# A two-layer decoder trunk on one core: all block inversions on POOL, value low parts on DVE, a recurrence in shorter hops

## The chip, the cores and the metric

One core of one Trainium2 chip runs the kernel. The metric is device time in microseconds of one execution, and lower is better; the time before is 2413.06 us, the median of 3 runs (2410.73 to 2416.13). The engines are PE (matrix products), DVE (vector), ACT (scalar functions), POOL (general) and SP, which here issues nearly all DMA transfers. Each engine has its own queue and works through it in order; an instruction that waits for a semaphore holds everything behind it on that engine.

## What is computed

The reference is a trunk of two layers over 512 tokens and 2048 channels, in float32. Layer 0 is forgetting attention (32 heads of 64), layer 1 is RWKV-7 time mixing with a state of 64x64 per head. Both have a gate by SiLU, an output projection and a residual. The part around the change is layer 1's recurrence:

```python
def step(S, inp):
    r_t, w_t, k_t, v_t, a_t, b_t = inp
    sa = jnp.einsum('bhvk,bhk->bhv', S, a_t)
    S = S * w_t[:, :, None, :] + sa[..., None] * b_t[:, :, None, :] \
        + v_t[..., None] * k_t[:, :, None, :]
    y_t = jnp.einsum('bhvk,bhk->bhv', S, r_t)
    return S, y_t
...
r, k, v, z = xr @ w_in[0], xk @ w_in[1], xv @ w_in[2], xg @ w_in[3]
v = v + (v_first - v) * jax.nn.sigmoid(v0 + (xv @ v1) @ v2)
...
return (y * jax.nn.silu(z)) @ w_out
```

The kernel does not step through 512 tokens. It works in chunks of 64 tokens. Within a chunk the dependence of the tokens on each other is a triangular 64x64 system per head, which is inverted beforehand; between chunks a state is handed on.

## The kernel before, in words

**Products.** Every large product is done in split precision: an operand is cut into a high part (`hi`, `whi`, made by ACT) and a low part (`lo`, `wlo`, made by DVE or POOL as source minus high part), and three streamed products replace one (high times high, low times high, high times low). Activations lie as 16 tiles of 128 channels x 512 tokens. An output tile of 128 channels takes 16 steps of 3 products into a PSUM bank `pj`. Its weights come in four parts of 4 steps (`raw`, 256 KB, three buffers; then `whi` and `wlo`, four buffers each), so one part feeds 12 products. SP loads a part, ACT and DVE split it, PE uses it.

**Layer 1's order on PE.** `backbone` (line 319) streams the output tiles: the rest of k, 16 of r, 16 of v (the values), 16 of z (the gate), 16 of the output projection. The first two tiles of each kind alternate. In what follows, V1 to V64 are the weight parts of the value tiles in the order of their use: V1 to V8 are tiles 0 and 1, V9 to V12 are tile 2, and so on.

**The planner.** `Flow` is a list of due tasks with a planned clock `fl.t`. Every PE product moves this clock on by its columns at 2400 per us (lines 91 to 96). All other work is written as tasks that run for a step, then `yield` how many units later the next step is due. So the program text of PE, DVE and ACT is laid down interleaved, in the order of the planned clock, and stays in that order on these three engines. SP's and POOL's queues are put in order by the framework's own scheduler, from the same text and its own notion of when something is ready.

**Mixed operands.** `mixed` (line 1114) makes the high and low part of one of the 16 activation tiles `hp` for the next kind of tile: `i` is 1 for r, 0 for the values, 2 for the gate. Line 1120 chooses the engine of the low part: for r and the values every second one goes to POOL.

**Inversions.** `keys` (line 1304) prepares one pair of heads, j = 0 to 15, and stores the triangular blocks to `mld`. After every fourth pair (a group, 4 in all) it starts `invert` and, later, `inverse` twice, for two pairs each. `invert` (line 1387) loads a group's 32x32 blocks as `lane`, one block per partition, and eliminates in 30 steps of two instructions (`lt`, then `lane`); POOL then masks, clears and stores the result to `qld`. In groups 0 to 2 POOL does the 30 steps in one go. Group 3 is in `DG`: DVE does them, spread over `DINV` = 32 units of the planner, and the two `inverse` tasks are due 40 and 52 units after the group's keys in place of 54 and 66. `inverse` (line 1409) reads `qld` back into `qt` (four loads on SP for each pair), turns blocks on DVE, joins them to 64x64 with small products on PE, and stores the result to `qtd`. The buffers of `qt` go round in fives.

**The recurrence.** `side` (line 1757) starts it when all 16 inverses are planned: `stage` loads the operands of two chunks (`rt`, `bk`, `prk`, `L`, `QP`, `SV`), `products` and `bonus` prepare them, and `recur` (line 1589) takes the 32 chunks of four groups of heads one after the other. A chunk is three hops: x from the state (copied by DVE to `xs`), times the inverse (copied by DVE to `SV`), then the new state (added by DVE). `hop` (line 1584) waits until the planned clock passes the next multiple of `HOP` = 3.9 units; between hops PE streams weights' products. `normed` finishes the output of two chunks and stores it to `ypd`, which the gate tiles read.

Of the kernel before, what the change touches and what calls it, by code (L numbers as in the profile page):

```python
# [12 lines left out]
OP = mybir.AluOpType  # L13
# [4 lines left out]
P = 128  # L18
# [113 lines left out]
def body(ctx, tc, a, out, dbg=None, stop=0):  # L132
    nc = tc.nc
    pe, act, dve, pool, sp = (InOrder(tc, e) for e in (nc.tensor, nc.scalar, nc.vector,
                                                       nc.gpsimd, nc.sync))
# [96 lines left out]
    def act_hi(hi, src):  # L232
        act.activation(hi, src, AF.Copy)
# [5 lines left out]
    def new_act(k):  # L239
        hi = cur["a"].tile([P, T], R, tag="hi", name="hi")  # L240
        lo = cur["a"].tile([P, T], R, tag="lo", name="lo")
        return hi, lo
# [46 lines left out]
    def silu_c(mp):  # L289
        cb = mp.tile([P, D], F, name="cb", bufs=1)  # L290
        cs = mp.tile([P, KT], F, name="cs", bufs=1)
        i = act.activation(cs, vecs[:, V_C], AF.Silu)
        return cb, cs, i
# [17 lines left out]
    def load(q, src, tag, shape=(P, T), bufs=None):  # L311
        t = q.tile(list(shape), F, tag=tag, name=tag, bufs=bufs)
        sp.dma_start(t, src)
        return t
# [81 lines left out]
    with ExitStack() as s0:  # L396
# [7 lines left out]
        with tc.tile_pool(name="st0", bufs=2, reuse_waits="tile") as q:  # L404
# [97 lines left out]
            cb, cs, i = silu_c(cbp)  # L502
# [95 lines left out]
        fl = Flow()  # L598
# [5 lines left out]
        q = sq0.enter_context(tc.tile_pool(name="at", bufs=2, reuse_waits="tile"))  # L604
# [318 lines left out]
        n = len(tiles)  # L923
# [112 lines left out]
    def col(v, j):  # L1036
        return vecs[:, v, j:j + 1]

    def c3(t):
        return t.rearrange("p (c t) -> p c t", c=NCH)  # L1040

    def u3(t):
        return t.rearrange("p (u t) -> p u t", u=NU)

    def of(d, j):

        return d[j // NJ][:, :, j % NJ]
# [3 lines left out]
    fl = Flow()  # L1051
# [7 lines left out]
    q = pools.enter_context(tc.tile_pool(name="kq", bufs=2, reuse_waits="tile"))  # L1059
# [24 lines left out]
    def need2(tag):  # L1084

        r = rings[tag]
        while any(r[i] > fl.t for i in range(max(0, len(r) - 2), len(r))):
            yield 0.1
        n = len(r)
        r[n] = r[n + 1] = 1e9  # L1090
        return n, n + 1

    def read(tag, n):
        rings[tag][n] = fl.t + 0.7
# [14 lines left out]
    def take(tag):  # L1109
        while not free[tag]:  # L1110
            yield 0.2
        free[tag] -= 1

    def mixed(i, to, old, k, m):
        while len(to) < k or k and (id(old), k - 1) not in spent:
            yield 0.1
        to.append(new_act(k))
        act_hi(to[k][0], m)
        yield 0.5
        e = pool if (k + 1) % (2, 2, 99)[i] == 0 else dve  # L1120
        e.tensor_tensor(out=to[k][1], in0=m, in1=to[k][0], op=OP.subtract)
        ready.add((id(to), k))
        free["m"] += 1
# [180 lines left out]
    def keys(q, j):  # L1304
        ip = q.tile([P, T], F, tag="ip", name="ip", bufs=2)
        sp.dma_start(u3(ip), of(ipd, j))
        kt = load(q, kTd[j], "kt", bufs=2)
        aa = load(q, aad[j], "aa", bufs=2)
        yield 8
        sq = q.tile([P, T], F, tag="sq", name="sq")  # L1310
        act.activation(sq, kt, AF.Square, scale=col(V_KK, j))
        yield from take("eI")
        eI = eIs[0]
        act.activation(eI[:, :, 1:], c3(ip), AF.Exp, scale=-EDEC)
        yield 2.2
        ss, n = yield from means(q, blkr, sq, "mh", "ml")
        yield 0.7
        t = q.tile([P, T], F, tag="t", name="t")
        act.activation(t, ss, AF.Relu, scale=2.0 ** 26, bias=nfloor)
        read("S", n)  # L1320
        act.activation(t, t, AF.Ln, bias=floor)
        act.activation(t, t, AF.Exp, scale=-0.5, bias=lnb)
        yield from take("eN")
        eN = q.tile([P, NCH, C], F, tag="eN", name="eN")
        act.activation(eN, c3(ip), AF.Exp, scale=EDEC)
        yield 2
        kk = q.tile([P, NCH, C], F, tag="kk", name="kk")
        dve.scalar_tensor_tensor(out=kk, in0=c3(kt), scalar=col(V_KK, j), in1=c3(t),
                                 op0=OP.mult, op1=OP.mult)
        at = q.tile([P, NCH, C], F, tag="at", name="at", bufs=2)  # L1330
        yield 0.7
        dve.scalar_tensor_tensor(out=at, in0=kk, scalar=-1.0, in1=eI[:, :, 0:C],
                                 op0=OP.mult, op1=OP.mult)
        free["eI"] += 1
        yield 0.7
        yield from take("bk")
        bk = q.tile([P, 2, NCH, C], F, tag="bk", name="bk")
        dve.tensor_tensor(out=kk, in0=kk, in1=c3(aa), op=OP.mult)
        yield 0.7
        dve.tensor_tensor(out=bk[:, 0], in0=kk, in1=eN, op=OP.mult)  # L1340
        yield 0.7
        act.activation(aa, aa, AF.Identity, scale=col(V_KA, j), bias=oka[:, j:j + 1])
        yield 0.8
        dve.tensor_tensor(out=kk, in0=c3(aa), in1=c3(kt), op=OP.mult)
        yield 0.7
        dve.tensor_tensor(out=bk[:, 1], in0=kk, in1=eN, op=OP.mult)
        free["eN"] += 1
        yield 1
        sp.dma_start(of(atd, j), u3(at.rearrange("p c t -> p (c t)")))
        for i in range(2):  # L1350
            sp.dma_start(bkd[j // NJ][:, :, i, j % NJ], u3(bk[:, i].rearrange("p c t -> p (c t)")))
        yield 1.5
        yield from take("gab")
        gab = q.tile([P, 2, 4, C], F, tag="gab", name="gab", bufs=12)
        ns = yield from need2("S")
        gs = [bank("S") for _ in ns]
        for c in range(4):
            for h in range(2):
                pe.matmul(gs[h][:, c * P:(c + 1) * P],
                          bk[HS[h], 0, 2 * c:2 * c + 2].rearrange("p c t -> p (c t)"),  # L1360
                          at[HS[h], 2 * c:2 * c + 2].rearrange("p c t -> p (c t)"),
                          start=True, stop=True)
        yield 0.7
        for h in range(2):
            g3 = gs[h].rearrange("p (c t) -> p c t", c=4)
            act.activation(gab[0:64, h], g3[0:64, :, 0:C], AF.Copy)
            act.activation(gab[64:128, h], g3[64:128, :, C:P], AF.Copy)
            read("S", ns[h])
            yield 0.7
        gabs[j] = gab  # L1370
        free["bk"] += 1
        yield 1.5
        for p in range(2):
            for b in range(2):
                r = 64 * p + 32 * b
                l = 32 * (j % 4) + 16 * p + 8 * b
                sp.dma_start(mld[j // 4, l:l + 8].rearrange("c s t -> s c t"),
                             gab[r:r + 32, :, :, 32 * b:32 * b + 32].rearrange(
                                 "s h c t -> s (h c) t"))
        md.add(j)  # L1380
        if j % 4 == 3:
            fl.start(fl.t + 1, invert(q, j // 4))
            for i in range(0, 4, 2):
                fl.start(fl.t + (DINV + 8 if j // 4 in DG else INV) + 6 * i,
                         inverse(q, (j - 3 + i, j - 2 + i)))

    def invert(q, grp):
        yield 3
        while not md >= set(range(4 * grp, 4 * grp + 4)):
            yield 0.2  # L1390
        m = q.tile([P, 32, 32], F, tag="lane", name="lane", bufs=2)
        sp.dma_start(m, mld[grp])
        for s in range(1, 31):
            n = 31 - s
            t = q.tile([P, s, n], F, tag="lt", name="lt")
            e = dve if grp in DG else pool
            e.tensor_tensor(out=t, in0=m[:, 0:s, s:s + 1].broadcast_to([P, s, n]),
                               in1=m[:, s:s + 1, s + 1:].broadcast_to([P, s, n]),
                               op=OP.mult)
            e.tensor_tensor(out=m[:, 0:s, s + 1:], in0=m[:, 0:s, s + 1:], in1=t,  # L1400
                            op=OP.add)
            if grp in DG:
                yield DINV / 30
        pool.affine_select(out=m, in_=m, pattern=[[-1, 32], [1, 32]],
                           compare_op=OP.is_ge, fill=0.0, base=-1, channel_multiplier=0)
        pool.memset(m.rearrange("p s t -> p (s t)")[:, 0:1024:33], 1.0)
        pool.dma_start(qld[grp], m)
# [176 lines left out]
    def hop():  # L1584
        n = fl.t // HOP
        while fl.t // HOP == n:
            yield 0.1
# [162 lines left out]


    STW = 5
    DG, DINV = (3,), 32
    HOP = 3.9
    INV, KEY = 54, 9.8

    def side(q):
# [102 lines left out]
```

## Time and profile before

| what | us |
|---|---|
| median of 3 runs | 2413.06 |
| the profiled execution, its own time | 2413.1 |
| its span, first to last instruction | 2411.2 |
| PE busy in the span | 2308.0 |
| DVE, ACT, POOL busy | 1605.5, 1257.2, 686.2 |
| granted clock of PE, mean | 0.982 |

A span is divided into what each engine does; an engine that is not the bottleneck may idle at no cost. In the profile nearly all instructions have line L90, since one helper records them, so they are told apart by their tiles (`out<-in`). A wait row reads: who waited, for whom, total us, times, longest. In a timeline row the first number is the start, the second the duration, and the square brackets hold the engine's idle time before it and what ended that. Some matmul records can be missing.

### The profile page before, as it was taken

What the parts mean: (1) busy time and instruction counts of PE and PEld (TensorE: products, weight loads), DVE (VectorE), ACT (ScalarE), POOL (GpSimd) and SP (SyncE); (2) the same over time, 40 slices, a digit from 0 to 9 for tenths busy, and PEclk for the clock granted to TensorE, in tenths of its full rate; (3) what the DMA queues carried; (4) which work ended last, traced back from release to release, by engine and by line L of the source; (5) the groups of instructions that cost most, each with busy time, mean ns of one, the idle gap of its engine ahead of it and who ended that gap; (6) DMA issues with size and microseconds to landing.
All of it is one profiled execution on the core that took longest, in us unless ns stands there. A gap on an engine that the chain in (4) does not pass through costs nothing. (4 is left out here: it accounts for less than half of the span.)

```text
span 2411.2 us, 39377 instructions
## 1 busy us (share of the span) xinstructions
PE 2308.0 (96%) x13626; PEld 1807.8 (75%) x13626; DVE 1605.5 (67%) x2850; ACT 1257.2 (52%) x2300; POOL 686.2 (28%) x1114
## 2 busy tenths in 40 slices
PE   6999899999999999998999898899999999999999
PEld 4787677877778778886777676677777777777787
DVE  6886678888888745335797567667477776765322
ACT  4435655555565544225646777764345556665221
POOL 0002332533324210110042207771245535450000
PEclk8999999999999999999999999989999999999999
DMA  8864366666666456444755999886867766644543
GB/s 304 329 224 158 108 198 216 212 216 222 201 222 213 133 181 205 137 147 141 227 183 185 301 270 278 262 253 192 237 184 198 212 177 189 173 132 153 160 137 96
DMA packets 388151, 480.22 MB, mean 199 GB/s; under 512 B 146032, under 2 KB 217840, under 8 KB 384112
## 3 DMA queue, kind: packets, MB, share of 16 engines
q1 hardware_dynamic: 386288, 475.08, 63.4%
q0 software_dynamic: 1664, 2.63, 0.3%
q8 instruction: 108, 1.77, 0.3%
q14 instruction: 91, 0.75, 0.1%
HBM read 381.63 MB, written 95.95 MB: 198 GB/s over the span
## 5 line engine op out<-in xcount | busy, mean ns | idle before, releaser
L90 PE MATMUL pj<-hi,whi 128*128 128x512 f32 x2416 | 987.5, 409 | 14.2 <-ACT hi L90 8.2
L90 PE MATMUL pj<-hi,wlo 128*128 128x512 f32 x2416 | 960.2, 397 | 9.1 <-DVE wlo L90 9.1
L90 PE MATMUL pj<-lo,whi 128*128 128x512 f32 x2416 | 960.1, 397 | 0.0
L90 DVE TENSOR_TENSOR wlo<-raw,whi 128x512 fp32r<-128x512 f32 (+2 forms) x628 | 474.5, 763 | 261.4 <-ACT whi L90 258.0
L90 ACT ACTIVATE whi<-raw 128x512 fp32r<-128x512 f32 (+2 forms) x628 | 394.2, 634 | 405.2 <-PE pj L90 229.3
L90 PEld LDWEIGHTS pj<-hi,whi 128*128 128x128 f32 x2416 | 459.6, 190 | 120.4 <-ACT hi L90 9.0
L90 PEld LDWEIGHTS pj<-lo,whi 128*128 128x128 f32 x2416 | 458.4, 190 | 108.7 <-DVE lo L90 0.6
L90 PEld LDWEIGHTS pj<-hi,wlo 128*128 128x128 f32 x2416 | 460.1, 190 | 105.1 <-DVE wlo L90 12.4
L90 DVE CUSTOM_DVE_ANT_0 wm<-wm,cb 128x1024 f32<-128x1024 f32 x128 | 156.7, 1225 | 0.3
L90 POOL TENSOR_SCALAR SV<-SV,dec 64x64 f32<-64x64 f32 x224 | 93.4, 439 | 105.9 <-DVE SV L90 71.7
L90 ACT ACTIVATE pr<-Sm,mx 128x128 f32<-128x128 f32 (+3 forms) x128 | 71.5, 558 | 85.6 <-POOL mx L90 81.6
L90 POOL TENSOR_SCALAR mx<-mx 128x1 f32<-128x1 f32 x128 | 65.7, 513 | 154.9 <-DVE mx L90 118.0
L90 POOL TENSOR_SCALAR pr<-pr,rc 128x128 f32<-128x128 f32 (+3 forms) x128 | 87.6, 685 | 33.0 <-DVE rc L90 28.6
L90 POOL TENSOR_TENSOR lt<-lane 128x30 f32<-128x30 f32 (+14 forms) x90 | 62.7, 697 | 83.9 <-DMA lane<-mld 77.1
L90 DVE CUSTOM_DVE_ANT_0 Sm<-S,cmask 128x128 f32<-128x128 f32 (+3 forms) x128 | 62.0, 484 | 36.0 <-PE S L90 35.4
L90 POOL TENSOR_TENSOR bk<-bk,eI 128x512 f32<-128x512 f32 x32 | 36.1, 1128 | 112.3 <-PE S L90 75.3
L90 POOL TENSOR_TENSOR lane<-lane,lt 128x30 f32<-128x30 f32 (+14 forms) x90 | 65.7, 730 | 7.1
L90 PE MATMUL S<-k,q 128*128 128x128 f32 (+7 forms) x256 | 62.4, 326 | 0.0
L90 PE MATMUL tr<-ident,pr 128*128 128x128 f32 x320 | 57.2, 277 | 4.3 <-DVE pT L90 1.4
L90 POOL TENSOR_TENSOR acc<-acc,sq 128x512 f32<-128x512 f32 x14 | 18.1, 1295 | 150.8 <-ACT sq L90 150.8
L90 PEld LDWEIGHTS tr<-ident,pr 128*128 128x128 f32 x320 | 41.6, 142 | 25.4 <-ACT pT L90 6.9
L90 DVE SCALAR_TENSOR_TENSOR hp<-pj,gate,hp 128x512 f32<-128x512 f32 x16 | 12.0, 751 | 68.9 <-PE pj L90 68.9
(325 smaller groups left out, 3272.8 us busy)
## 6 DMA issues: line engine op xcount, KB each, us to landing
wm<-in_wmodT SPq DMA_DIRECT2D x132, 512.0 KB, 4.3
raw<-in_wz SPq DMA_DIRECT2D x128, 256.0 KB, 3.8
raw<-in_wo SPq DMA_DIRECT2D x128, 256.0 KB, 3.5
raw<-in_wv SPq DMA_DIRECT2D x124, 256.0 KB, 3.8
wm<-in_wmodT SPq DMA_DIRECT2D x30, 1024.0 KB, 6.9
raw<-in_wk SPq DMA_DIRECT2D x96, 256.0 KB, 3.7
raw<-in_wr SPq DMA_DIRECT2D x64, 256.0 KB, 5.1
raw<-in_wq SPq DMA_DIRECT2D x56, 256.0 KB, 3.6
```

The source lines that it names most:

```text
L90: self.last = f(*a, **k)
```

## The change

Three things change. Every group's inversion is done by POOL in one go, so the table `DG`, its spread `DINV` and the shorter due time of group 3's inverses are gone; these are due 54 and 66 units after the keys, like the other groups'. The low parts of the values' operand are all made on DVE; r's are still shared. And `HOP` is 3.6 units in place of 3.9.

```diff
@@ mixed
-        e = pool if (k + 1) % (2, 2, 99)[i] == 0 else dve
+        e = pool if i == 1 and k % 2 else dve
@@ keys
-                fl.start(fl.t + (DINV + 8 if j // 4 in DG else INV) + 6 * i,
-                         inverse(q, (j - 3 + i, j - 2 + i)))
+                fl.start(fl.t + INV + 6 * i, inverse(q, (j - 3 + i, j - 2 + i)))
@@ invert
-            e = dve if grp in DG else pool
-            e.tensor_tensor(out=t, in0=m[:, 0:s, s:s + 1].broadcast_to([P, s, n]),
+            pool.tensor_tensor(out=t, in0=m[:, 0:s, s:s + 1].broadcast_to([P, s, n]),
                                in1=m[:, s:s + 1, s + 1:].broadcast_to([P, s, n]),
                                op=OP.mult)
-            e.tensor_tensor(out=m[:, 0:s, s + 1:], in0=m[:, 0:s, s + 1:], in1=t,
-                            op=OP.add)
-            if grp in DG:
-                yield DINV / 30
+            pool.tensor_tensor(out=m[:, 0:s, s + 1:], in0=m[:, 0:s, s + 1:], in1=t,
+                               op=OP.add)
@@ constants
-    DG, DINV = (3,), 32
-    HOP = 3.9
+    HOP = 3.6
```

Two places of the new order follow. First DVE, where group 3's inversion begins; `lo` is a low part of the values' operand, `wlo` of a weight part. Before:

```order
L90 TENSOR_TENSOR wlo<-raw,whi 128x512
L90 TENSOR_TENSOR lt<-lane 128x30
L90 TENSOR_TENSOR lane<-lane,lt 128x30
L90 TENSOR_TENSOR lo<-hp,hi 128x512
L90 TENSOR_TENSOR wlo<-raw,whi 128x512
L90 TENSOR_TENSOR lt<-lane 128x58
L90 TENSOR_TENSOR lane<-lane,lt 128x2x29
L90 TENSOR_TENSOR lt<-lane 128x84
L90 TENSOR_TENSOR lane<-lane,lt 128x3x28
L90 TENSOR_TENSOR lo<-hp,hi 128x512
```

Now:

```order
L90 TENSOR_TENSOR wlo<-raw,whi 128x512
L90 TENSOR_TENSOR lo<-hp,hi 128x512
L90 TENSOR_TENSOR wlo<-raw,whi 128x512
L90 TENSOR_TENSOR lo<-hp,hi 128x512 x2
L90 TENSOR_TENSOR wlo<-raw,whi 128x512
```

The 60 steps are gone from DVE and stand in one piece on POOL, right behind group 2's store to `qld`, where eight `lo` stood; those eight are now on DVE.

Second SP, around group 3's reads of `qld`. `qt_13171` and `qt_13174` are the buffers of pairs 12 and 13 here, `qtd<-qt_13174` and `qtd<-qt_13177` store pairs 8 and 9, and the three `raw` in the first row are V8 to V10. Before:

```order
L90 DMA raw<-in_wv 128x512 x3
L90 DMA qtd<-qt_13174 128x512
L90 DMA qtd<-qt_13177 128x512
L90 DMA hp<-mxd 128x512 x3
L90 DMA raw<-in_wv 128x512
L90 DMA qt_13171<-qld 32x8x32 x4
L90 DMA qt_13174<-qld 32x8x32 x4
L90 DMA sv<-svd 128x512
L90 DMA raw<-in_wv 128x512 x2
```

Now:

```order
L90 DMA raw<-in_wv 128x512 x3
L90 DMA qtd<-qt_13174 128x512
L90 DMA qtd<-qt_13177 128x512
L90 DMA qt_13171<-qld 32x8x32 x3
L90 DMA raw<-in_wv 128x512 x2
L90 DMA qt_13171<-qld 32x8x32
L90 DMA qt_13174<-qld 32x8x32 x4
L90 DMA qt_13177<-qld 32x8x32
L90 DMA sv<-svd 128x512
L90 DMA raw<-in_wv 128x512
```

V11 stood ahead of the first read of `qld` and stands behind it now, though the same inverse is due later on DVE, where its first turned block moves from behind V13's low part to behind V17's.

On PE the recurrence's first product with `QP` stands 60 streamed products later than before, and the last step of its last chunk 69 earlier.

## The prediction

> **What bounds the kernel now.** I read the page first, then the chain of waits, then the waits of the matmul engine (PE) by stretch, then each engine's timeline where the change acts. The page's list of engines:
>
> ```profile
> PE 2308.0 (96%) x13626; PEld 1807.8 (75%) x13626; DVE 1605.5 (67%) x2850; ACT 1257.2 (52%) x2300; POOL 686.2 (28%) x1114
> ```
>
> The last long piece of the chain of waits (start, length, what, how many):
>
> ```profile
> 2237.22 170.14 PE pj L90 x728
> ```
>
> PE is busy 96% of 2411.2 us, and the change gives PE as many rows as before, 10,262, so only PE's pauses can change: 103 us in all. Undisturbed, a streamed product (128x512, into bank pj) costs 170.14/728 = 0.234 us. Three stretches matter: the last group's inversion (1612 to 1660), the recurrence (1735 to 2203), the end of the gate tiles (2203 to 2238). One or more rows of PE's waits from each, in that order (total us, times, longest):
>
> ```profile
> PE pj L90 <- DVE wlo L90: 6.1, 4, 1.7
> ```
>
> ```profile
> PE S L90 <- ACT GP L90: 8.3, 5, 4.1
> PE S L90 <- ACT mhi L90: 3.9, 1, 3.9
> ...
> PE x L90 <- DVE SV L90: 0.9, 1, 0.9
> PE x L90 <- DVE xs L90: 0.6, 1, 0.6
> ```
>
> ```profile
> PE pj L90 <- DVE wlo L90: 3.0, 4, 1.4
> ```
>
> In the inversion PE waits for DVE. In the recurrence it waits mostly for ACT emptying score banks, and only 0.9 + 0.6 us for the recurrence's own copies (SV, xs). Busy time by stretch, with columns stretch, length, then PE, weight loads, DVE, ACT, POOL, granted clock, DMA share, GB/s:
>
> ```profile
> 1617.00:1629.00 12.00, 8.95 (x26) 6.49 (x26) 11.62 (x25) 3.88 (x8) 3.07 (x3) 0.72 0.76 247
> 1640.00:1652.00 12.00, 8.24 (x85) 5.67 (x84) 11.53 (x26) 4.65 (x9) 1.42 (x1) 0.86 0.63 178
> 1652.00:1677.00 25.00, 25.00 (x287) 20.14 (x286) 15.39 (x35) 10.54 (x22) 2.29 (x4) 1.00 0.75 207
> 1735.00:2203.00 468.00, 450.98 (x4374) 352.96 (x4374) 320.23 (x683) 264.43 (x455) 207.47 (x394) 0.99 0.63 176
> ```
>
> In the first two DVE is full, PE pauses 3.05 and 3.76 us, and the clock falls: half clock for (1-0.72)x2 = 56% of 12 us is 6.7 us, and (1-0.86)x2 of 12 is 3.4. In the third PE never pauses. In the recurrence it pauses 17 us.
>
> **Part 1: the last inversion and half the low parts change places.** What DVE loses, on its timeline:
>
> ```profile
> 1616.55 0.19 DVE L90 TENSOR_TENSOR lt<-lane 128x30 f32<-128x30 f32 x1 [10.02 <-DMA lane<-mld]
> ...
> 1617.48 1.76 DVE L90 TENSOR_TENSOR wlo<-raw,whi 128x512 fp32r<-128x512 f32 x1
> ```
>
> and on PE's:
>
> ```profile
> 1619.30 0.50 PE L90 MATMUL pj<-hi,wlo 128*128 128x512 f32 x1 [1.38 <-DVE wlo L90]
> ...
> 1621.94 0.80 PE L90 MATMUL pj<-hi,wlo 128*128 128x512 f32 x1 [1.67 <-DVE wlo L90]
> ...
> 1623.38 0.63 PE L90 MATMUL pj<-hi,wlo 128*128 128x512 f32 x1
> 1623.81 0.63 PE L90 MATMUL pj<-lo,whi 128*128 128x512 f32 x1
> ```
>
> DVE's queue is in order. Its first inversion instruction waits 10.02 us for the lane load, with the weights' low part (wlo) behind it; PE then stops at 1619.30 and 1621.94. After that products start 0.43 us apart instead of 0.234, so 6.7 us of half clock hold about 15 products and cost 15x0.2 = 3.0 us; 3.4 us cost 1.5. Stage total: 3.05 + 3.76 + 3.0 + 1.5 = 11.3 us. It is of DVE's making: the block, 60 small instructions, and a wlo that takes 1.76 us while a low part runs on POOL. In the change DVE carries 16 low parts there and no inversion. I take 11 us as removed up to 1652 (bounds 5, if weight loads that come late there stay late, and 11.3).
>
> **Where it goes next.** The inversion now lasts as long as POOL makes it, and SP waits for its result. The tile `lane` (minimum/median/maximum ns, first and last start; the last row is its loads and stores):
>
> ```profile
> L90 DVE TENSOR_TENSOR lt<-lane x30: 191/329/1497, 1616.5 to 1657.5; 128x30 f32<-128x30 f32 x2, 128x58 f32<-128x58 f32 x2, 128x84 f32<-128x84 f32 x2, 128x108 f32<-128x108 f32 x2
> ...
> DMA to landing us min/median/max: 5.1/6.0/7.8
> ```
>
> POOL's timeline, first step and end of groups 0 and 2:
>
> ```profile
> 1455.62 0.24 POOL L90 TENSOR_TENSOR lt<-lane 128x30 f32<-128x30 f32 x1 [69.70 <-DMA lane<-mld]
> ...
> 1505.54 1.60 POOL L90 TENSOR_SCALAR_AFFINE_SELECT lane<-lane 128x1024 f32<-128x1024 f32 x1
> ...
> 1565.93 0.23 POOL L90 TENSOR_TENSOR lt<-lane 128x30 f32<-128x30 f32 x1 [7.38 <-DMA lane<-mld]
> ...
> 1610.66 1.26 POOL L90 TENSOR_SCALAR_AFFINE_SELECT lane<-lane 128x1024 f32<-128x1024 f32 x1
> ```
>
> SP's waits from 1611 to 1700, and its queue:
>
> ```profile
> SPq L90 <- DMA qld<-lane: 4.4, 2, 3.0
> ```
>
> ```profile
> 1657.74 1.11 SPq L90 DMA_DIRECT2D qtd<-qt  x2
> ...
> 1664.92 3.78 SPq L90 DMA_DIRECT2D qt<-qld  x8
> 1668.79 0.40 SPq L90 DMA_DIRECT2D sv<-svd  x1
> 1669.29 0.86 SPq L90 DMA_DIRECT2D raw<-in_wv  x2
> ```
>
> POOL takes 1505.5-1455.6 = 49.9 us for group 0 and 44.7 for group 2. Group 3 starts when the lane data is there, 1616.5 as now. I take group 2's 44.7, nearest in time and in DVE's load: 1661.2; then 1.26 for the masking and 0.5 (taken) for a clearing and the store's issue; the store to qld 5.1, the least, as DMA is light while SP waits: landed at 1668.1. Bounds: DVE's own length now, 41.2, gives 1664.6; 49.9 and a store of 7.8 give 1676. Now it lands at 1664.9, when SP's wait of 3.0 us ends.
>
> Most of this inverse is emitted 14 planner units later, but the order shows that SP's first three reads of qld are not: they stand one weight load EARLIER, ahead of part V11 (the third part of value tile 2's weights). SP stores qtd as soon as PE and ACT have done group 2's first pair, 11 us before 1657.74, and then stands at qld for some 20 us with V11 and all later loads behind it. PE, 11 us ahead, runs dry. The rows for that: PE's first product of V11, a high part on ACT, DVE's product with sv for value tile 1, and the page's row of these loads (KB, us to landing).
>
> ```profile
> 1676.70 0.40 PE L90 MATMUL pj<-hi,whi 128*128 128x512 f32 x1
> ```
>
> ```profile
> 1668.27 0.63 ACT L90 ACTIVATE whi<-raw 128x512 fp32r<-128x512 f32 x1
> ```
>
> ```profile
> 1671.65 0.69 DVE L90 TENSOR_TENSOR vf<-vf,sv 128x512 f32<-128x512 f32 x1 [0.67 <-DMA sv<-svd]
> ```
>
> ```profile
> raw<-in_wv SPq DMA_DIRECT2D x124, 256.0 KB, 3.8
> ```
>
> PE starts V11 at 1676.70 now. In the change: landing 1668.1, three reads at 3.78/8 = 1.4 us, load 3.8, high part 0.63, low part 0.69 (a DVE pass of that shape), 0.3 between them: 1674.9. Without the wait PE would come at 1676.7-11 = 1665.7, so it stands for 9.2 us; of the 11 us only 1.8 remain. The clock falls after such a pause, and between the 3.0 and 1.5 above I take 1.8. Sum of part 1: -11 + 9.2 + 1.8 = 0. Bounds: -4.5 (landing 1664.6, so 5.7 stood, clock 0.8) and +9 (landing 1676, 17.1 stood, clock 3.0). V12 has a second wait before it: the load sv for value tile 1 comes after six more reads, and DVE's product with sv stands ahead of V12's low part. Landing 1668.1, nine reads 4.3, two weight loads 0.9, sv 2.9 (1668.79 to 1671.65), two DVE passes 1.4: 1677.6, when PE needs it (1674.9 + 12x0.234 = 1677.7). Nothing more is lost there.
>
> The rows of wlo beside an inversion on POOL (1455 to 1505) and without one (1660 to 1735), and one POOL step twice:
>
> ```profile
> L90 DVE TENSOR_TENSOR wlo<-raw,whi x14: 691/1038/1192, 1454.3 to 1504.6; 128x512 fp32r<-128x512 f32 x14
> ```
>
> ```profile
> L90 DVE TENSOR_TENSOR wlo<-raw,whi x23: 678/692/710, 1660.6 to 1733.0; 128x512 fp32r<-128x512 f32 x23
> ```
>
> ```profile
> 1587.55 0.62 POOL L90 TENSOR_TENSOR lt<-lane 128x240 f32<-128x240 f32 x1
> ...
> 1589.03 0.95 POOL L90 TENSOR_TENSOR lt<-lane 128x240 f32<-128x240 f32 x1
> ```
>
> Some 30 low parts in the stage cost DVE 0.35 us more each, 10 us beside the 21 of the passes themselves, in 44 us: no path. The other way round, POOL's step is 0.62 or 0.95 us. Once SP holds the loads back DVE has nothing to do, and POOL's last 20 us shrink by up to a third, 6 us: landing at 1662, rival B. [...]
>
> **Part 2: the recurrence.** It starts 60 products later and ends 69 earlier in PE's order (1,047 products between its steps become 918). Its second product, first and last start:
>
> ```profile
> L90 PE MATMUL x<-xs,QP x512: 221/222/369, 1754.1 to 2188.4; 128*64 128x64 f32 x171
> ```
>
> 31 chunks take 434.3 us, so one of a chunk's 3 hops takes 4.67 us; 3.6/3.9 of it is 4.31, and DVE has 0.36 us less to answer. It is late in only 2 of some 95 steps now (0.9 and 0.6). I take the same again, +1.5; bounds 0 (nothing gets late) and +9 (a quarter of 95 steps lose 0.36). The other 15 us there come from ACT's queue, where the exponentials of 16 stages stand for their loads; there are still 16: 0, bounds -6 and +6. The earlier end cannot give more than the 3.0 us lost after 2203, and that wait falls in the last gate tiles, after the recurrence is over: 0.
>
> **Sum.** The profiled execution took 2413.1 us (span 2411.2 and 1.9 around it), like the median 2413.06. 2413.1 + 0 + 1.5 = 2414.6; I say 2414.5.
>
> **Rivals.** *A, the stage's gain stays whole:* the wait at qld does not bind, because weights are loaded further ahead of PE than I count. For: PE does not pause from 1652 to 1677 though SP waits 3.0 us there. Against: three load buffers and four split ones hold seven parts, 84 products, 20 us, and part of them is used up when SP's wait begins. 2413.1 - 11 + 1.5 = 2403.6. Chance 0.15.
>
> *B, POOL runs free while DVE is empty:* landing at 1662, PE stands 9.2-6.1 = 3.1 us, clock 1: 2413.1 - 11 + 3.1 + 1 + 1.5 = 2407.7. For: the 0.62 row. Against: over half of the inversion is done before DVE empties. Chance 0.17.
>
> *C, slower, SP is held longer:* one mechanism, SP's wait for qld; from a landing at 1668 on every us is a us of PE. With group 0's 49.9 and a 7.8 us store it is +9, and with 1.5 for the hops 2423.6; the middle of the case is 2421. For: group 0 took that long. Against: DVE had more to do then. Chance 0.17.
>
> *D, slower, the shorter hop decides:* once a quarter of the steps miss, +9, 2422. For: DVE is busy 320 of 468 us there. Against: two late steps of 95 now. Chance 0.11.
>
> **How the numbers follow.** Forecast, no change: 0.40. A measurement of this kernel tells 0.2% (4.8 us) from no change. Faster: A and B, 0.32, of which 0.03 fall within 0.2%: 0.29. Slower: C and D, 0.28. Within: 0.43. The likeliest case alone: 2409 to 2419. The range for 8 in 10 reaches from below A to above C and D: 2402 to 2425.
>
> **What would show it.** Right: SP's wait for qld<-lane grows to over 10 us; PE pauses 5 to 10 us between 1660 and 1676 on whi or wlo; no pause of PE from 1617 to 1650; DVE's block of 10.02 us is gone. Wrong: qld lands before 1660, or PE runs through that stretch (A, B); PE's waits for xs and SV pass 5 us (D). I would also be wrong if ACT's stands in the recurrence changed by over 6 us, which the order does not settle.

## The result and the profile after

The change takes 2431.93 us (median of 4 runs, 2430.28 to 2432.96), before 2412.93 beside it: ratio 1.0085, 95% interval 1.0073 to 1.0097. It is 19 us slower, outside the predicted range of 2402 to 2425. The profiled execution took 2431.0 us, span 2429.0. PE, from the page:

```profile
PE 2313.1 (95%) x13626; PEld 1813.1 (75%) x13626; DVE 1600.1 (66%) x2798; ACT 1255.8 (52%) x2300; POOL 712.2 (29%) x1166
```

PE has the same instructions as before, yet it is busy 5.1 us longer (a slower clock, 0.980 in place of 0.982) and pauses 115.9 us in place of 103.2, 12.7 more. Both together are the 17.8 us by which the span grew. Busy time by stretch says where (columns as in the prediction: stretch, length, PE, weight loads, DVE, ACT, POOL, granted clock, DMA share, GB/s):

```profile
1617.00:1629.00 12.00, 11.23 (x49) 8.80 (x48) 8.65 (x10) 6.92 (x13) 10.74 (x17) 1.00 0.82 273
1640.00:1652.00 12.00, 12.00 (x163) 9.32 (x163) 6.19 (x9) 4.25 (x11) 10.77 (x16) 0.87 0.56 142
1652.00:1677.00 25.00, 20.75 (x201) 16.70 (x200) 9.97 (x16) 7.58 (x16) 7.98 (x17) 0.86 0.52 144
1735.00:2203.00 468.00, 437.44 (x4292) 339.79 (x4291) 324.86 (x686) 257.59 (x444) 211.93 (x403) 0.97 0.62 171
2203.00:2238.00 35.00, 35.00 (x152) 28.20 (x151) 17.71 (x32) 18.88 (x30) 0.00 (x0) 1.00 0.56 176
```

In the stage of the last inversion DVE is no longer full, and PE's loss has moved to the third row. The recurrence carries the result: PE pauses 468-437.4 = 30.6 us there, 17.0 before, and the clock is 0.97 in place of 0.99. After 2203 the 3.0 us of pauses are gone.

**The stage.** PE's waits from 1612 to 1677:

```profile
PE x L90 <- ACT us L90: 4.2, 1, 4.2
PE pj L90 <- ACT r L90: 2.8, 1, 2.8
PE pj L90 <- DVE wlo L90: 1.8, 3, 0.8
```

The timelines of SP, ACT and PE where the longest of them ends:

```profile
1663.43 1.31 SPq L90 DMA_DIRECT2D qt<-qld  x3
1664.83 0.87 SPq L90 DMA_DIRECT2D raw<-in_wv  x2
```

```profile
1668.47 0.63 ACT L90 ACTIVATE whi<-raw 128x512 fp32r<-128x512 f32 x1 [6.41 <-DMA raw<-in_wv]
1669.13 0.78 ACT L90 ACTIVATE us<-x 32x256 f32<-32x256 f32 x2
```

```profile
1669.55 1.46 PE L90 MATMUL x<-qt,us 32*32 32x32 f32 x32 [4.16 <-ACT us L90]
```

And SP's wait for the inverse, from 1600 to 1700:

```profile
SPq L90 <- DMA qld<-lane: 10.7, 1, 10.7
```

Up to ACT's `whi` this is the predicted chain: SP stands at `qld` until 1663.43, makes three reads, and only then issues V11. ACT's high part of V11 waits 6.41 us for it, with the copy `us` behind it in ACT's queue, and PE waits for `us`.

**The recurrence.** PE's waits from 1735 to 2203, and its second product per chunk:

```profile
PE S L90 <- ACT vt L90: 11.1, 3, 4.7
PE S L90 <- DVE mlo L90: 5.5, 6, 2.0
PE S L90 <- DVE vf L90: 5.0, 2, 4.1
PE x L90 <- DVE xs L90: 2.9, 2, 1.9
PE S L90 <- ACT GP L90: 2.7, 4, 1.2
PE S L90 <- ACT sq L90: 1.0, 2, 0.7
PE x L90 <- DVE SV L90: 0.9, 2, 0.7
```

```profile
L90 PE MATMUL x<-xs,QP x512: 221/222/271, 1768.7 to 2194.9; 128*64 128x64 f32 x171
```

The waits for DVE sum to 14.3 us, before to 3.8 (`SV` 0.9, `xs` 0.6, and two rows that the prediction does not show):

```profile
PE S L90 <- DVE mlo L90: 1.8, 4, 0.6
```

```profile
PE S L90 <- DVE vf L90: 0.5, 1, 0.5
```

Those for ACT are 14.8, before 12.2. A hop takes (2194.9-1768.7)/93 = 4.58 us, not 4.31; before it took 4.67. All of the waits for `mlo` and `vf` in the change fall in the first half of the stretch, while the value tiles still run. That half, before and then in the change:

```profile
1735.00:1969.00 234.00, 220.23 (x2170) 172.37 (x2170) 174.22 (x365) 120.29 (x222) 111.15 (x212) 0.97 0.72 195
```

```profile
1735.00:1969.00 234.00, 209.63 (x1989) 161.69 (x1989) 168.03 (x346) 110.23 (x204) 106.77 (x202) 0.95 0.67 181
```

PE pauses 24.4 us there in place of 13.8, although DVE is busy for less time than before, 168.0 us in place of 174.2. What DVE did ahead of the longest wait for it:

```profile
1893.65 1.42 DVE L90 SCALAR_TENSOR_TENSOR prk<-rt,vecs,bk 64x128 f32<-64x128 f32 x4
1895.10 0.88 DVE L90 COPY SV<-x 64x256 f32<-64x256 f32 x2
1896.01 0.71 DVE L90 SCALAR_TENSOR_TENSOR prk<-rt,vecs,bk 64x128 f32<-64x128 f32 x2
1896.75 1.14 DVE L90 SCALAR_TENSOR_TENSOR dc<-dc,vecs,sq 128x128 f32<-128x128 f32 x4
1897.81 1.14 DVE L90 SCALAR_TENSOR_TENSOR dc<-dc,vecs,bv 128x128 f32<-128x128 f32 x4
...
1902.74 0.69 DVE L90 TENSOR_TENSOR vf<-vf,pj 128x512 f32<-128x512 f32 x1
```

```profile
1903.57 1.09 PE L90 MATMUL S<-ident,vf 128*128 128x128 f32 x4 [4.09 <-DVE vf L90]
```

From 1892 to 1904 DVE works with hardly a gap, through recurrence copies, side work of the stages (`prk`, `dc`) and a value tile (`vf`), while PE waits at the head of its own queue for the last of it. Such a run is not by itself what stops PE: the kernel before has a longer one, and PE works right through it.

```profile
1783.00:1805.00 22.00, 22.00 (x233) 17.56 (x232) 21.30 (x45) 11.16 (x21) 13.77 (x27) 1.00 0.75 198
```

### The profile page after: what moved, and what is told of

It is laid out like the page before. It is cut to its first block, busy times and chain, and to the rows that moved or that the text cites. A ratio compares the mean times of both kernels' runs of the same rounds, so it can differ in the third digit from the quotient of the medians.

```text
span 2429.0 us, 39369 instructions
## 1 busy us (share of the span) xinstructions
PE 2313.1 (95%) x13626; PEld 1813.1 (75%) x13626; DVE 1600.1 (66%) x2798; ACT 1255.8 (52%) x2300; POOL 712.2 (29%) x1166
## 5 line engine op out<-in xcount | busy, mean ns | idle before, releaser
L90 POOL TENSOR_TENSOR lt<-lane 128x30 f32<-128x30 f32 (+14 forms) x120 | 81.6, 680 | 90.9 <-DMA lane<-mld 81.7
L90 POOL TENSOR_TENSOR lane<-lane,lt 128x30 f32<-128x30 f32 (+14 forms) x120 | 85.9, 715 | 9.4
L90 DVE TENSOR_TENSOR lo<-hp,hi 128x512 fp32r<-128x512 f32 x54 | 43.4, 809 | 36.2 <-ACT hi L90 34.9
```

Source lines behind the costliest of these rows:

```text
L90: self.last = f(*a, **k)
```

## The experiments

All are read against the kernel before, run beside them on the same chip. The differences are of medians; the change itself stands at +19.0.

| run | what differs | us | against before | ratio, 95% |
|---|---|---|---|---|
| e1 | before, hop 3.6 | 2427.47 | +15.2 | 1.0041 to 1.0067 |
| e2 | change, hop 3.9 | 2443.90 | +31.7 | 1.0112 to 1.0138 |
| e3 | before, low parts on DVE | 2409.60 | -2.6 | 0.9977 to 0.9996 |
| e4 | before, inversion on POOL, later start | 2447.36 | +35.1 | 1.0126 to 1.0154 |
| e5 | change less 64 us of DVE work | 2412.49 | +1.1 | 0.9993 to 1.0013 |
| e6 | before less the same 64 us | 2403.70 | -7.7 | 0.9954 to 0.9979 |
| e7 | before, later start alone | 2438.86 | +27.4 | 1.0103 to 1.0138 |
| e8 | change, hop 3.7 | 2434.09 | +22.7 | 1.0085 to 1.0115 |
| e9 | change, 8 gate low parts on POOL | 2432.84 | +21.9 | 1.0076 to 1.0103 |
| e10 | e3, 29 us of DVE work done by POOL | 2428.69 | +17.8 | 1.0055 to 1.0087 |
| e11 | e3, hop 3.75 | 2421.44 | +10.5 | 1.0028 to 1.0053 |
| e12 | e3, hop 4.05 | 2431.61 | +20.7 | 1.0076 to 1.0103 |
| e13 | change less 46 us (`prk`) | 2415.88 | +5.1 | 1.0010 to 1.0028 |
| e14 | change less 18 us (`dc`) | 2420.08 | +9.3 | 1.0024 to 1.0051 |
| e15 | change, hop 3.9, old start | 2413.36 | +2.6 | 1.0005 to 1.0024 |

### Which of the parts: e1 to e4

e1 is the kernel before with the short hop; e2 the changed kernel with the old one, the same two lines the other way round:

```diff
-    HOP = 3.9
+    HOP = 3.6
```

e3 is the kernel before with the low parts on DVE; in e4, which is e2 otherwise, this line is the old one again:

```diff
-        e = pool if (k + 1) % (2, 2, 99)[i] == 0 else dve
+        e = pool if i == 1 and k % 2 else dve
```

> The kernel before with nothing changed but the hop, 3.6 planner units apart in place of 3.9 (start of the recurrence, inversions and low parts as before). The traces say that up to the recurrence the two kernels are level and that the 19 us arise inside it: from product 5283 to 6600 PE's pauses grow from 20.0 to 30.6 us and what it loses at half clock from 6.9 to 14.2 us. Theory H, the shorter hop is the cause: +15 to +19 us against before. Rival I, the later start is the cause (the side work of the recurrence is squeezed at its start): within 4 us of before. Rival O, each new order of the side work falls differently: anything from -10 to +15.

> The changed kernel with the hop back at 3.9 units; inversions on POOL, low parts on the vector engine and the later start stay. Theory H: within 4 us of before (part 1 by itself came out level in the traces: PE loses 36.5 us from product 4700 to 5283 before and 36.7 after). Rival I: +15 to +19 us, as the full change. Rival O: anything from -10 to +15.

> The kernel before with only the low parts of the values operand all on the vector engine. PE's order is the same row for row, so only DVE's load and POOL's move. In the prediction this part had no price of its own. [...] All theories of the recurrence: no change there.

> The kernel before with only the last group's inversion on POOL and the later start that goes with it; hop 3.9, low parts as before. Theory H: within 5 us of before. Rival I: +15 to +19. Beside the all-but-hop kernel it tells what the low parts are worth once DVE has no inversion: the same within 2 us, since DVE then has room (the wait for the weights' low part went from 6.1 to below 2 us in the stage).

Measured +15.2, +31.7, -2.6 and +35.1. Theory H holds for the hop alone and falls as the whole cause: without the short hop the rest of the change is worse still, and worse than either theory expected of e2 and e4. So the parts work against each other. e3 gained. Before, the `wlo` at 1617.48 took 1.76 us while a low part ran on POOL (1617.30, 1.40 us); the median `wlo` from 1616 to 1660 took 0.69. With all low parts on DVE, PE's wait for `wlo` in the stage went from 6.1 to 4.4 us. Why a pass takes longer beside one on the other engine no run shows. With the inversion on POOL the low parts are worth 3.4 us (e4 less e2), a little more than the 2 us allowed. The hop alone shows the same pattern in the recurrence as the change, PE's busy time and the two largest waits:

```profile
1735.00:2203.00 468.00, 437.67 (x4283) 339.65 (x4282) 317.26 (x682) 259.66 (x449) 209.98 (x396) 0.97 0.61 172
```

```profile
PE S L90 <- DVE mlo L90: 8.2, 11, 1.4
PE S L90 <- DVE vf L90: 5.7, 2, 4.3
```

### The later start: e7, e12

e7, on the kernel before:

```diff
-                fl.start(fl.t + (DINV + 8 if j // 4 in DG else INV) + 6 * i,
+                fl.start(fl.t + INV + 6 * i,
```

e12, on e3:

```diff
-    HOP = 3.9
+    HOP = 4.05
```

> The kernel before with only the inverse of the last group scheduled at the later time (54 units in place of 40); the inversion itself stays on the vector engine, hop 3.9. Theory S, the later start alone is what cost 32 to 35 us in the two kernels with hop 3.9: the recurrence now ends at product 6426 instead of 6354 and PE stands some 15 us at product 6481 for the gate tile that needs its output: +20 to +33 us. Rival P, the inversion on POOL costs them: within 5 us of before.

> The kernel before with the low parts on DVE and a hop of 4.05: the recurrence starts where it did (product 5307) and ends at 6420. If the end decides what the later start cost (PE's stand of 15 us at product 6481, 17 us of half clock), this start must cost it too: +12 to +24 us against 2409.6, with the stand on the gate tile in the trace. If the start itself is what costs, no stand and -5 to +3 us, a longer hop being easier on DVE.

Measured +27.4 and +20.7, the second 23 above e3. In e7 the inversion is still on DVE and the hop still 3.9, so the start costs this by itself. In e12 the recurrence starts where it always did and only ends later (product 6420), and it pays too: the late end is a good part of the cost. PE's longest wait, what ACT stood for, and the time at half clock, in e7:

```profile
2255.82 0.80 PE L90 MATMUL pj<-hi,whi 128*128 128x512 f32 x1 [15.12 <-ACT z L90]
```

```profile
ACT L90 <- DMA gd<-z: 12.3, 1, 12.3
```

```profile
2243.00:2260.00 17.00, 4.18 (x10) 3.33 (x11) 3.50 (x8) 3.73 (x5) 0.00 (x0) 0.50 0.54 174
```

The last gate tiles multiply by the recurrence's output. They hold their buffers until it comes, ACT cannot empty the next bank, and PE, whose next product needs that bank, stands for 15.1 us. The clock is half for 17 us, but most of that lies inside the stand; PE works at half speed for only the 4.2 us behind it. In e12 the same wait:

```profile
2244.13 0.79 PE L90 MATMUL pj<-hi,whi 128*128 128x512 f32 x1 [13.16 <-ACT z L90]
```

The end is not all of it. In e7 PE also pauses 27.9 us from 1735 to 2203, 17.0 before; in e12 23.5, 15.7 in e3. And though e12's hop is longer, which was expected to be easier on DVE, PE's waits for `mlo` there are 7.6 us, 1.8 in e3:

```profile
PE S L90 <- DVE mlo L90: 7.6, 8, 1.9
```

So a recurrence that is moved against the other work can make DVE late without being denser.

The change starts as late as e7 (product 5367, e7 5376) but ends at 6285, and has no such stand. Its short hop buys this, at the price of e1.

### The price of the short hop: e5, e6, e13, e14

These four kernels leave out part of what is computed. e13 takes the first of these passes out of the change, e14 the second, e5 both; e6 takes both out of the kernel before:

```diff
-                dve.scalar_tensor_tensor(out=prk[s, j], in0=rt[s, j],
-                                         scalar=vecs[s, V_RK, NJ * g + j:NJ * g + j + 1],
-                                         in1=bk[s, j, :, 1 - h, :], op0=OP.mult, op1=OP.mult)
```

```diff
-            dve.scalar_tensor_tensor(out=dc[:, s], in0=dc[:, s], scalar=col(V_LB, NJ * g + j),
-                                     in1=bv[:, s], op0=OP.add, op1=OP.add)
```

> The changed kernel without the bonus products (prk keeps the loaded decay, 8 instructions of 0.36 us a stage) and without the last bias-and-bonus pass over dc (4 of 0.29 us a stage): 16 x 4.0 = 64 us of DVE left out inside the recurrence, the order of every engine otherwise kept. Theory D, at hop 3.6 DVE is too full for the side work (PE's waits on DVE in the recurrence: 3.8 us before, 14.3 in the change, 17 with the hop alone): the waits on DVE go below 5 us, half clock goes with them, -12 to -18 us against the full change. Rival R, PE waits for ACT behind late loads (vt behind a weight part: 11.1 us in the change): less than 5 us gained.

> The kernel before without the same 64 us of DVE work (bonus products, last pass over dc), so that the change's gain from it can be read beside this one. Theory D: hop 3.9 leaves DVE enough room, its waits are only 3.8 us, so -2 to -5 us. Rival R: the same small gain as in the change.

> The full change without the bonus products alone (prk keeps the loaded decay; 16 x 8 x 0.36 = 46 us of DVE left out); the last pass over dc stays. If DVE's time in all counts, its share of the 19.5 us that leaving out 64 us gave: 46/64, so -12 to -16 us. If the way from rt to prk to the bonus product on PE counts (a latency ahead of mhi and mlo), nearly all: -17 to -20. If the pass over dc counts: -3 or less.

> The full change without the last pass over dc alone (bias and bonus; 16 x 4 x 0.29 = 18 us of DVE left out, after which only a store waits); the bonus products stay. If DVE's time in all counts: 18/64 of 19.5, -4 to -7 us. If the latency of the prk way counts: -2 or less.

Against the full change's +19.0, e5 gained 17.9 us and e13 13.9, as theory D and DVE's time expected; e14 gained 9.7, more than the 4 to 7 expected. e6 gained 7.7 against before, more than the 2 to 5 expected. In e5 the recurrence reads (stretch; PE's one wait for DVE that is left; second product):

```profile
1735.00:2203.00 468.00, 448.96 (x4369) 350.93 (x4368) 262.10 (x511) 267.33 (x458) 213.47 (x402) 0.99 0.63 177
```

```profile
PE S L90 <- DVE mlo L90: 0.6, 1, 0.6
```

```profile
L90 PE MATMUL x<-xs,QP x512: 222/222/271, 1769.0 to 2177.2; 128*64 128x64 f32 x171
```

The waits for DVE fall from 14.3 to 0.6 us, the clock returns to 0.99, and a hop takes (2177.2-1769.0)/93 = 4.39 us, close to the predicted 4.31. The waits for ACT stay, so rival R falls. The gains go with PE's waits for DVE: 14.3 us in the change, 8.0 in e14, 3.9 in e13, 0.6 in e5. So DVE's side work is what keeps the short hop from being short. About 10 of the 19 us are the change's own (17.9 less the 7.7 that the kernel before gains too; each gain is known to 3 or 4 us). The other 9 remain when both kernels are without this work (e5 +1.1, e6 -7.7); part 1 is 2.6 of them (e15 below), and the rest was not followed. It is not the way through `prk` by itself, since leaving out `dc`, on which no product of the recurrence waits, gave 9.7. Nor does it look like a plain sum of DVE's time: 18, 46 and 64 us left out gave 9.7, 13.9 and 17.9, the first ones most, though a proportional 5 for e14 lies only just outside its interval. What fixes which microseconds of DVE count was not settled, and in the next two runs moving DVE work to POOL did not help.

### Relief without leaving work out: e9, e10

e9, on the change:

```diff
-        e = pool if i == 1 and k % 2 else dve
+        e = pool if i and k % 2 else dve
```

e10, on e3:

```diff
-        dve.tensor_tensor(out=vv, in0=vv, in1=sv, op=OP.mult)
+        pool.tensor_tensor(out=vv, in0=vv, in1=sv, op=OP.mult)
-            dve.scalar_tensor_tensor(out=dc[:, s], in0=dc[:, s], scalar=col(V_LB, NJ * g + j),
-                                     in1=bv[:, s], op0=OP.add, op1=OP.add)
+            pool.tensor_scalar(dc[:, s], dc[:, s], col(V_LB, NJ * g + j), 1.0,
+                               op0=OP.add, op1=OP.mult)
+        pool.tensor_tensor(out=dc, in0=dc, in1=bv, op=OP.add)
```

> The full change with every second low part of the gate operand (8 of 16, tile lo, 0.7 us each on DVE from 1905 to 1948 us) on POOL in place of DVE; PE's and ACT's order is the same row for row, and everything is computed. Theory D (DVE is too full beside the denser recurrence): the relief lies where PE waited 6.9 us for DVE (4.1 on vf, 2.0 and 0.8 on mlo, 1903 to 1938), so -4 to -9 us with the half clock behind it. Rival R (PE waits for ACT behind late loads): within 2 us of the full change. [...]

> The kernel before with the low parts of the values operand on DVE (2.6 us gained by themselves) and 29 us of DVE work of the recurrence done by POOL: the values' product with sv (16 x 0.69) and the last pass over dc (16 x 4 x 0.29, as four additions of the bias and one of the bonus). Theory D: leaving out 64 us gave 7.7, so these 29 give 2 to 4 more: 2405 to 2408. [...]

Theory D's figures failed in both. e9 is the same as the change within its interval, as rival R had it: the longest wait on `vf` went from 4.1 to 3.6 us and others moved, and the waits for DVE sum to 14.3 us as in the change, although eight passes (5.5 us) were gone from DVE. This does not bring R back, since e5 removed DVE's waits, left ACT's, and gained 17.9. e10 lost 20 us against e3, where theory D expected a gain of 2 to 4. The largest waits of SP and PE and ACT's wait for weights in its recurrence:

```profile
SPq L90 <- POOL dc L90: 54.9, 17, 7.7
```

```profile
PE S L90 <- ACT GP L90: 14.6, 9, 4.6
```

```profile
ACT whi L90 <- DMA raw<-in_wv: 27.0, 10, 7.0
```

The product with `sv` takes 1.29 us on POOL, 0.69 on DVE, and DVE's next step waits for it (20.9 us in all). SP now stands 54.9 us for POOL's `dc` (30.8 for DVE's in e3) with later loads behind it, ACT waits 27.0 us for weights, 7.0 at the longest (8.1 and 3.3 in e3), and PE's largest wait is for ACT, 8.0 us in e3. The product moved to POOL left DVE free but came out later. That in-order queues then carry the delay to PE fits these rows, but the way from one to the next was not followed: in e5 ACT waits 29.6 us for weights without such a loss.

### Hops between, and the first part by itself: e8, e11, e15

e8 is the change with `HOP = 3.7`, e11 is e3 with `HOP = 3.75`. e15 is the change with `HOP = 3.9` and

```diff
-                fl.start(fl.t + INV + 6 * i, inverse(q, (j - 3 + i, j - 2 + i)))
+                fl.start(fl.t + (40 if j // 4 == 3 else INV) + 6 * i, inverse(q, (j - 3 + i, j - 2 + i)))
```

> The full change with hop 3.7 in place of 3.6. Its recurrence starts at product 5373 and ends at 6336 (5367 and 6285 at 3.6; 5376 and 6426 at 3.9). If two smooth costs work against each other, a denser recurrence and a later end, then with the end before product 6354 the stand at the gate tiles is absent and the density lies between: 2422 to 2428 us. Rival O, each order falls differently: anywhere from 2415 to 2445.

> The kernel before with the low parts on DVE and a hop of 3.75 (start at product 5334, end at 6315). Theory D as a smooth cost: half way between 2409.6 (3.9) and about 2425 (3.6, less 2.6 for the low parts): 2414 to 2420. Rival O, each order falls differently: below 2410 or above 2424.

> The full change with hop 3.9 and the last group's inverse scheduled at 40 units, as before: PE's order and the place of the recurrence are those of the kernel before (4 swaps of names aside), only the last inversion is on POOL and the low parts on DVE. It shows part 1 with nothing of part 2. PE's first products of this inverse now stand for qld directly: by the trace of the change qld lands at 1663.4, where PE comes to them at about 1650 with the DVE block gone, so some 13 us of stand against the 11 us that the block cost: -4 to +8 us against before. If the inversion on POOL were itself the loss of the full change: +15 or more.

With the old start, hops of 4.05, 3.9, 3.75 and 3.6 stand at +20.7, -2.6, +10.5 and +15.2 (e1 has not the low parts on DVE, worth 2.6). So 3.9 lies in a hollow among those tried: a longer hop ends too late, and below 3.9 the price rises as the hop shrinks, most of it in the first half of the way. With the later start, 3.9, 3.7 and 3.6 stand at +31.7, +22.7 and +19.0. e8 came 6 us and e11 1.4 us above the upper ends of their expectations, so the two costs do not add up smoothly. What is left of rival O, that each new order falls differently, was not separated from the density.

e15 shows part 1 with the recurrence in its old place: +2.6 us, and against e3 +5.2. PE's waits in the stage, 1612 to 1677:

```profile
PE x L90 <- ACT us L90: 3.8, 2, 3.7
PE pj L90 <- ACT r L90: 2.9, 1, 2.9
```

These are the change's two stands; the 13 us at `qld` that were expected did not come. So the inversion on POOL costs about 5 us where it stands, the low parts on DVE give back 2.6, and neither is what made the change slow.

## Why the prediction was wrong

**Right: what can change.** Same instructions, so pauses and the clock behind them; the whole difference is there.

**Near in sum, wrong in its terms: part 1.** Predicted 0 (-4.5 to +9), measured +2.6. That the sum came out near is luck: both large terms were about twice too big. *What was removed* was not 11 us but about 5: the product that starts at 1613.23 before starts at 1612.08 in the change, and the one at 1670.10 at 1663.91. That is the lower bound, but not for the reason given with it: up to 1652 PE still pauses 0.8, 0.6, 2.8 and 0.5 us, the 2.8 being a new wait for ACT's `r`, and has 3.1 us of half clock (0.87 over 12 us) in place of 10.1. *Where it went next* came as written at SP, with V11 behind `qld`, but SP stood 10.7 us there, not some 20, and PE 4.16 us, not 9.2. PE stood at a joining product behind ACT's `whi`, not at V11's own product, which starts at 1676.95 (1676.70 before).

With the measured landing, 1663.4, and the measured lead of 6.2 us the prediction's steps give no stand at V11 at all (ready at 1663.4+6.8 = 1670.2, PE there at 1676.7-6.2 = 1670.5). What it left out is the copy `us` behind `whi` in ACT's queue, for which an earlier product waits. The landing came 4.7 us before the predicted 1668.1, as the tile `lane` shows:

```profile
L90 POOL TENSOR_SCALAR_AFFINE_SELECT lane<-lane x4: 1265/1265/1271, 1503.8 to 1658.7; 128x1024 f32<-128x1024 f32 x4
```

```profile
DMA to landing us min/median/max: 2.9/6.6/8.2
```

The masking began 2.5 us earlier than taken (1661.2) and a store landed in 2.9 us, below the 5.1 that before had as its least. The claim of no pause from 1617 to 1650 was wrong.

**The step that failed: part 2, "it is late in only 2 of some 95 steps now ... I take the same again, +1.5".** The hop alone costs 15.2 us (e1). That count took in only the recurrence's own copies, `xs` and `SV`. They did go from 1.5 to only 3.8 us, below the 5 that was set as D's sign. But the same DVE queue also makes each stage's `mlo` and each value tile's `vf`, and PE waits for these at the head of its queue: 2.3 us before, 10.5 now. The prediction had put these 2.3 us down to ACT with "the other 15 us there", of which ACT's rows are 12.2. DVE's busy share, 320 of 468 us, which it held for D, could not have told it either: in the first half DVE is less busy in the change than before, and PE waits for it more. That DVE's work is what holds PE up is shown by e5, for about 10 of the 19 us; why it comes out late, by density or by the new order, stays open. The 31 chunks took 426.2 us, where 31x3x4.31 = 400.8 was forecast. Between the first and last second product:

```profile
1769.00:2195.00 426.00, 400.34 (x4070) 311.08 (x4065) 302.12 (x639) 241.51 (x416) 200.89 (x386) 0.98 0.61 170
```

PE pauses 25.7 us of these; before, in a stretch of 435 us from 1754, it was 12.3. The forecast hop was scaled from a time that already held pauses, as if they would shrink with it. The clock was left out of this term altogether.

**A term that was missing: the later start.** "It starts 60 products later and ends 69 earlier" was quoted, and the end was priced at 0 with at most 3.0 us to gain; it gave these 3.0. But the start had no price. With the old hop it costs 27 us (e7), about half of it by the stand at the end; the change avoids that stand only by its short hop. For the change itself the term stays small: e1's 15.2 and e15's 2.6 leave 1.2 of the 19.0 for it, less than these differences are known to.

**The rivals.** A, B and C were about `qld` and did not decide; the landing at 1663.4 lies near B's 1662 (with 6 us off POOL's time, an estimate from steps of 0.62 and 0.95 us), but B's gain needed the 11 us removed, and 5 were. D named the right part and the right engine, with the wrong place (the recurrence's copies) and too small a size (+9, where the pauses alone grew by 13.6). The ACT stands changed by 2.6 us, within the 6 allowed. Predicted within 0.2%: it was 0.85% slower.

## What to carry to other kernels

When a dependent chain is packed closer, price everything its in-order engines make for the bottleneck engine, not just the chain's own copies. The rows to read are the bottleneck's waits for that engine, all of them: the engine's busy share did not tell here, and neither did the length of its runs without a gap. Look also for the consumer that runs dry when a chain ends late; here 70 products more at its end cost 15 us of standing. Moving work to an idle but slower engine (before, a low part took POOL 1.40 us and DVE 0.68, medians from 1590 to 1670) did not pay in e9 and cost 20 us in e10. Of all full versions only the low parts on DVE (e3) beat the kernel before, by 2.6 us (0.9977 to 0.9996), and that is less than 0.2%.

## What the runs showed of the hardware

Here a pause could cost PE more than its length, and its length did not say how much. In the change, four 8 us stretches around pauses of 2.8 (ending 1786.7), 4.1 (1903.6), 4.7 (1762.8) and 2.0 us (1927.4):

```profile
1786.00:1794.00 8.00, 7.32 (x57) 5.97 (x58) 5.81 (x12) 4.02 (x9) 4.57 (x9) 0.57 0.57 151
1902.00:1910.00 8.00, 6.43 (x46) 5.17 (x46) 5.70 (x12) 2.01 (x4) 3.89 (x8) 0.57 0.76 220
1762.00:1770.00 8.00, 7.17 (x66) 5.59 (x67) 6.41 (x17) 2.98 (x6) 0.49 (x1) 0.79 0.58 155
1926.00:1934.00 8.00, 6.62 (x70) 5.25 (x71) 7.71 (x18) 3.59 (x7) 0.75 (x1) 1.00 0.47 139
```

Read by half microseconds, the clock around these pauses is 1.00 or 0.50, save where it changes; at 0.50 products start 0.43 us apart (1789.28 to 1790.98), at 1.00 0.23. So 0.57 over 8 us is (1-0.57)x2x8 = 6.9 us at half clock, the same for two pauses of different length; 0.79 is 3.4 us, for the longest of the four; and none came with the pause of 2.0 us. In the kernel before, two pauses of 1.4 and 1.7 us close together (1619.30 and 1621.94) came with 6.7 us. So in these places the half clock came in steps of about 3.4 us. What sets off such a step no run shows: a pause of 2.8 us came with 6.9 us, one of 4.7 us with 3.4.
